# Storing the low part of the attention keys twice over, so that both products of a score contract over 128 rows

## Chip, cores, metric

One NeuronCore of a Trainium2 chip. The metric is the device time of one execution in microseconds (us), from runs of the same program; lower is better.

## What is computed

Two transformer blocks over 256 tokens of width 1024, with 256 context tokens in the first block, followed by eight routed experts. The parts that this change touches are the scores of every attention in it:

```python
# block 1, two layers: 8 query heads, 2 key heads; latents see 512 keys, context tokens 256
s = jnp.einsum('bqkgd,bskd->bkgqs', q_blk, k).astype(jnp.float32) * scale
p = jax.nn.softmax(s, axis=-1).astype(v.dtype)
# block 2, first layer (DSA): index scores choose 64 keys for each query, then attention over them
rel = jax.nn.relu(jnp.einsum('bqhd,bsd->bqhs', iqb, ik))
s = jnp.einsum('bqgrd,bqkgd->bgrqk', qg, kg).astype(F32) * scale
# block 2, second layer (NSA): compressed, selected and windowed keys, each with its own softmax
sc = jnp.einsum('bgrqd,bngd->bgrqn', qb, kc).astype(F32) * scale
ss = jnp.einsum('bgrqd,bgqnld->bgrqnl', qb, kg).astype(F32) * scale
sw = jnp.einsum('bgrqd,bkgd->bgrqk', qb, kwb).astype(F32) * scale
```

All inputs are float32 and heads are 64 wide. Everything else (projections, convolution and state scan, feed-forward layers, experts) is not changed.

## The kernel before

The program is one straight line: layer 0 and layer 1 of block 1, then the DSA layer with its feed-forward, then the NSA layer, then the experts, which run from about 1850 us to the end. Each stage streams its weights by DMA from the SP queue into `raw` tiles; ScalarE rounds a tile to float32r (L363) and VectorE subtracts to get the low part (L364), so that each float32 product is done as three float32r matmuls (L369 to L371).

Scores are done in the same spirit with two matmuls. `query_stack` puts a query's high part on rows 0 to 63 and its low part on rows 64 to 127 of one stationary tile `qS`. `put_keys` (and `keys` in `block1_mixer` for block 1) makes two tiles of key columns: `kSa`, 128 rows, the high part twice over, and `kSb`, 64 rows, the low part. For each head the first matmul (L643) contracts all 128 rows, which gives high times high plus low times high; the second (L644) takes rows 0 to 63 of the query and `kSb`, which adds high times low:

```python
nc.tensor.matmul(sb[:, j * nk:(j + 1) * nk], q, ka, start=mask is None, stop=False)
nc.tensor.matmul(sb[:, j * nk:(j + 1) * nk], q[0:64], kb, start=False,
                 stop=mask is None or j == hb - 1)
```

The same pair stands at L1302 and L1304 in `dsa` (index scores) and at L1562 and L1563 in `nsa` (scores of 16 compressed keys, with tiles `kca` and `kcb`). A pair has as many columns as the head has keys in that tile: 512, 256, 128 or 16. The heads of one bank follow each other, so the 128-row and the 64-row matmuls alternate.

After the scores of a bank VectorE takes the negated maximum of each row (L647), ScalarE the exponentials with their sums (L652), TensorE transposes the probabilities (L660), one of ScalarE and VectorE copies them out of the bank (L130, L132), and TensorE multiplies them with the values (L670). `pipeline` traces these stages some units apart, so that TensorE has other banks' work between a unit's scores and its transposes. In block 1 the units of attention are merged with those of the convolution and of the state scan; in the DSA and NSA layers they stand mostly alone.

The order of each engine's instructions is made by the tile framework's scheduler from the order of tracing; nothing around the change has a hand-made order, except that the index scores and the choice of keys (`best`, L1315 to L1321) are traced with high priority.

Of the kernel before, what the change touches and what calls it, by code (L numbers as in the profile page):

```python
# [10 lines left out]
F32 = mybir.dt.float32  # L11
# [7 lines left out]
D = 1024  # L19
# [62 lines left out]
class Split:  # L82
    """the two parts of split data, in two tiles: [:, part, ...]"""
# [8 lines left out]
class Prog:  # L92
# [41 lines left out]
    def fill(self, n=1):  # L134
        """trace the next n steps of the conditioning products; parts of a step add up"""
        self.credit += n
        while self.credit >= 1 and self.fillers:
            if next(self.fillers[0], "end") == "end":
                self.fillers.pop(0)
            self.credit -= 1  # L140
# [7 lines left out]
    def settle_fillers(self):  # L148
        """to the end of a product that has begun"""
        if self.fillers and inspect.getgeneratorstate(self.fillers[0]) == inspect.GEN_SUSPENDED:  # L150
            self.drain(self.fillers[0])

    def pipeline(self, units, lag):
        """units: lists of stages; stage j of a unit is traced some units after stage j - 1"""
# [8 lines left out]
    @staticmethod  # L163
    def along(units, step, ahead):
        """step is traced with the first stage of a unit well before the last"""
        u = units[max(0, len(units) - ahead)]
        first = u[0]

        def both():
            first()  # L170
            step()
        u[0] = both

    @staticmethod
    def merge(a, b):
        """two lists of units as one, evenly mixed"""
# [81 lines left out]
    def matvec_pe(self, w, c0, st, nd, dest, bname, boff):  # L258
        """1024 columns on the tensor engine: four column groups, two halves by the parity of k"""
# [22 lines left out]
    def matvec_dve(self, w, c0, st, nd, dest, bname, boff):  # L282
        """2048 columns for one condition or 1024 for two: products and sums over k on the vector engine,
        over partitions on the tensor engine, four column groups at once"""
# [41 lines left out]
    def in_turn(self, name, op, after=None):  # L326
        """op is issued behind the last one of the name"""
# [7 lines left out]
    def in_order(self, within=False):  # L335
        """what is traced within is issued in that order, engine by engine, behind what was traced before unless within"""
# [12 lines left out]
    def unit(self, view, a, b, raw=None, after=None):  # L349
        """a float32 weight tile [128, a * b], in DRAM or (raw) already on chip, as two float32r parts [128, a, b]"""  # L350
# [22 lines left out]
    def lin_tok(self, xT, tiles, w, n, fill=0):  # L373
        """xT(k, tile) -> (hi, lo) [128, 128]; w: [units, 128, k per unit * n] in DRAM; one bank per token tile"""
# [18 lines left out]
    def rstd(self, ss, n, inv_n):  # L393
        """[128, n] sums of squares -> (ss * inv_n + eps) ** -0.5"""
# [16 lines left out]
    def split_evac(self, hi, lo, src, scale=None, bias=None, keep=None):  # L411
        """hi, lo <- src * scale + bias, split"""
# [14 lines left out]
    def rs32(self, ss):  # L427
        """[128, 2] sums of squares of the halves of rows of D -> a 32nd of the rows' (mean square + eps) ** -0.5"""
# [14 lines left out]
    def prenorm(self, xs, dests):  # L443
        """rows of a few token tiles, with their squares in self.ssx, normalised and transposed;
        dests: (A, shift, hT, column), where the split columns times A plus shift go"""
# [25 lines left out]
    def diagonal(self, x, r=None):  # L471
        """the identity times the factors of the rows' norm"""
# [5 lines left out]
    def settle_pair(self, xs, srcs, row, post, w0):  # L478
        """settle for the two token tiles that end a stage, the diagonals for their norms and the next stage's first
        weight tile, in the order in which the engines run them"""  # L480
# [49 lines left out]
    def settle(self, x, src, row, post):  # L530
        """residual row tile x += the two halves in src, normalised when post, times the gate row; and its squares"""
# [16 lines left out]
    def slot(self):  # L548
        """16 KB per partition: half of a split input"""
        return self.hp.tile([128, 4096], F32R, name="h")  # L550

    def split_cols(self, k=8, n=512):
        """[:, part, k, column]"""
        return Split([self.slot()[:, :k * n].rearrange("p (k n) -> p k n", k=k) for _ in range(2)])

# [9 lines left out]
    def rope_tabs(self, dst, cos, sin, w=None, scale=1.0):  # L565
        """dst [128, 2, 64]: factors of x and of x with its halves swapped"""
# [10 lines left out]
    def rope(self, dst, src, H, tab, out=None):  # L577
        """src [128, H, 64] -> dst, or out, with dst as scratch"""
# [8 lines left out]
    def key_stacks(self, pool, H, n):  # L587
        return (pool.tile([128, H, n], F32R, name="kSa"), pool.tile([64, H, n], F32R, name="kSb"))

    def put_keys(self, pool, kS, d, H, t):  # L590
        """keys [128 tok, H, 64] -> columns of token tile t: high part twice over, and low part"""
        nc = self.nc
        st = pool.tile([128, H, 3, 64], F32R, name="kst")
        nc.scalar.copy(st[:, :, 0], d)
        nc.vector.tensor_sub(st[:, :, 2], d, st[:, :, 0])
        nc.vector.tensor_copy(st[:, :, 1], st[:, :, 0])
        st = st.bitcast(F32)
        pa, pb = self.bank("tr", 2), self.bank("tr", 2)
        for h in range(H):
            nc.tensor.transpose(pa[:, h * 128:h * 128 + 128], st[:, h, 0:2].rearrange("p a d -> p (a d)"), self.ident)  # L600
            nc.tensor.transpose(pb[0:64, h * 128:h * 128 + 128], st[:, h, 2], self.ident)
        sl = slice(t * 128, t * 128 + 128)
        nc.scalar.copy(kS[0][:, :, sl], pa[:, :H * 128].rearrange("p (h n) -> p h n", h=H))
        nc.vector.tensor_copy(kS[1][:, :, sl], pb[0:64, :H * 128].rearrange("p (h n) -> p h n", h=H))

    def query_stack(self, pool, d, H):
        """queries [128 tok, H, 64] -> [high; low] columns, [128, H, 128 tok]"""
# [13 lines left out]
    def attention(self, H, nk, q_of, k_of, v_of, mask, o_of, sums, finish):  # L621
        """softmax(q k) v for one tile of 128 queries and H heads: units of stages; unnormalised columns of 64 in a bank"""
# [9 lines left out]
    def attention_group(self, g, hb, nk, nkt, q_of, k_of, v_of, mask, o_of, sums):  # L632
# [3 lines left out]
        def scores():  # L636
# [4 lines left out]
            for j in range(hb):  # L641
                q, (ka, kb) = q_of(g + j), k_of(g + j)
                nc.tensor.matmul(sb[:, j * nk:(j + 1) * nk], q, ka, start=mask is None, stop=False)  # L643
                nc.tensor.matmul(sb[:, j * nk:(j + 1) * nk], q[0:64], kb, start=False,  # L644
# [29 lines left out]
    def to_mixT(self, mixT, k0, t, x, scale=None, diag=None):  # L674
        """x [128 tok, 512], times the factors of its rows in diag -> split feature columns k0..k0+3 of token tile t"""
# [18 lines left out]
    def block1_mixer(self, l, hT, mix_fill, scope):  # L694
# [16 lines left out]
        with tc.tile_pool(name=f"mix{l}", bufs=1) as big:  # L711
            xT = lambda k, t: (hT[:, 0, k, t * 128:t * 128 + 128], hT[:, 1, k, t * 128:t * 128 + 128])

            # rope tables of the two latent tiles, with the norm weights in them
# [10 lines left out]
            # q, k, v, z  # L725
# [23 lines left out]
            def keys():  # L749
# [18 lines left out]
                lo = self.wk(4, 2, 64).bitcast(F32R)  # L768
                for tp in range(2):
                    k2 = kk[:, 2 * tp:2 * tp + 2]  # L770
                    hi = self.wk(4, 2, 64).bitcast(F32R)
                    hv = hi.rearrange("p (t h) c d -> p t h c d", t=2)
                    nc.scalar.copy(hv[:, :, :, 0], k2)
                    nc.vector.tensor_sub(lo[:, 2 * tp:2 * tp + 2], k2, hv[:, :, :, 0])
                    nc.vector.tensor_copy(hi[:, :, 1], hi[:, :, 0])
                    pa, pb = self.bank("tr", 2), self.bank("tr", 2)
                    for j in range(4):
                        c = slice(128 * j, 128 * j + 128)
                        nc.tensor.transpose(pa[:, c], hi.bitcast(F32)[:, j].rearrange("p a d -> p (a d)"), self.ident)
                        nc.tensor.transpose(pb[0:64, c], lo.bitcast(F32)[:, 2 * tp + j // 2, j % 2], self.ident)  # L780
                    for copy, dst, src in ((nc.scalar.copy, kS[0], pa), (nc.vector.tensor_copy, kS[1], pb[0:64])):
# [20 lines left out]
            # x, B, C through the convolution, and dt  # L802
# [45 lines left out]
            # attention: latent queries see context and latents, context queries the context  # L848
# [51 lines left out]
    def softplus(self, d, n):  # L900
        """d [128, n] in place: max(d, 0) + log(1 + exp(-|d|)), the logarithm as 2 atanh(u / (2 + u))"""
# [14 lines left out]
    def ssd_decay(self, l, big, dv):  # L916
        """step widths, their products with A, and the exponentials of the sums of these: shared tiles, filled by steps()"""
# [28 lines left out]
    def ssd(self, l, big, xs_tok, b_tok, bT, cT, outs):  # L946
# [58 lines left out]
        def chain(i, t, first):  # L1005
            """what the incoming state adds to chunk t, and the state it leaves"""
# [67 lines left out]
    def lin_wide(self, xT, groups, w, kt, after, fill=0, between=None):  # L1074
        """groups of two token tiles of x @ w, 1024 wide, in two banks each; the last units tile by tile;
        between is traced when the first half of the first group has been"""
# [24 lines left out]
    def out_proj(self, xT, groups, w, xs, rows, post, nxt, between=None, w0=None):  # L1101
        """x @ w, normalised when post, times its gate row, added to the residual; then nxt of each group"""
# [10 lines left out]
    def gate_rows(self, pool, mod, j, w, conds):  # L1113
        """gate times w times 32, along the rows; w None: the gate alone"""
# [12 lines left out]
    def ffn(self, name, xs, hT, w_gate, w_up, w_down, row_fn, post, fills, order, nxt, need=(), w0=None):  # L1127
        """residual += gate * (norm of) swiglu; order: pairs of token tiles, as they become ready; nxt of each pair"""
# [78 lines left out]
    def positions_tables(self):  # L1207
        """cos and sin of position * frequency; the angle is brought to [-pi, pi] first"""
# [30 lines left out]
    def heads_out(self, dst, o_bank, coef, add=None):  # L1239
        """dst = o * coef per head of 64 (+ dst)"""  # L1240
# [17 lines left out]
    def dsa(self, hT):  # L1258
# [4 lines left out]
        with tc.tile_pool(name="dsa", bufs=1) as big:  # L1263
# [15 lines left out]
            with tc.tile_pool(name="dsa_i", bufs=1) as bi:  # L1279
# [12 lines left out]
                def index(t):  # L1292
                    """index scores, the 64 best keys of each query, and the mask they leave"""
# [5 lines left out]
                    for g in range(0, 8, hb):  # L1299
                        sb = self.bank()  # L1300
                        for j in range(hb):
                            nc.tensor.matmul(sb[:, j * nk:(j + 1) * nk], qS[:, g + j], ikS[0][:, 0, :nk],  # L1302
                                             start=True, stop=False)
                            nc.tensor.matmul(sb[:, j * nk:(j + 1) * nk], qS[0:64, g + j], ikS[1][:, 0, :nk],  # L1304
# [58 lines left out]
    def att_job(self, mixT, t, hf, q_of, prep, branches, first=None):  # L1363
        """eight query heads of one token tile over some branches of keys: the sum of coef * attention"""
# [30 lines left out]
    def compress(self, big, which, src):  # L1395
        """src [128, 2, 256]: tokens of four heads -> hidden units, [128, 2 (256), 4 heads, 16 blocks], in three steps"""
# [53 lines left out]
    def nsa(self, hT, ahead):  # L1450
# [5 lines left out]
        with tc.tile_pool(name="nsa", bufs=1) as big:  # L1456
            kv = [big.tile([128, 2, 512], F32, name=f"kv{i}") for i in range(3)]
            kS = [None, self.key_stacks(big, 4, 256), (big.tile([128, 4, 256], F32R, name="kSa2"),
                                                       big.tile([64, 4, 256], F32R, name="kSb2"))]
            kcS = (big.tile([128, 64], F32R, name="kca"), big.tile([64, 64], F32R, name="kcb"))  # L1460
# [24 lines left out]
            def compressed_keys():  # L1485
# [5 lines left out]
                nc.vector.tensor_sub(kcS[1], b[0:64, 0:64], kcS[0][0:64])  # L1491
# [626 lines left out]
```

## Time and profile before

| | |
|---|---|
| timed runs | 2838.80, 2838.01, 2832.42 us; median 2838.01 |
| profiled execution | span 2838.7 us, first to last instruction (the page gives no other time for it) |
| TensorE (PE) busy | 2742.1 us, 97% |
| its weight loads (PEld) | 2230.8 us, 79% |
| VectorE (DVE), ScalarE (ACT) busy | 2099.1 us (74%), 1528.1 us (54%) |
| mean granted TensorE clock | 0.959 of full speed |

PE's busy time counts a matmul from its start to the modelled end of its pipeline, and successive matmuls overlap, so 97% says that there is nearly always a matmul under way, not that the array works at its peak. The distance from one matmul's start to the next one's start tells how fast they go. The granted clock has two levels, 1.00 (2.4 GHz) and 0.50 (1.2 GHz); a stretch's number is the mean over it.

### The profile page before, as it was taken

The numbers are of one execution on the slowest core, as the hardware profiler recorded it, in microseconds if no ns is written. First come the engines' busy times: TensorE is split into PE (matmuls) and PEld (weight loads), VectorE is DVE, ScalarE is ACT, GpSimd is POOL, SyncE is SP. The second block draws the span as 40 slices with busy tenths as digits, with TensorE's granted clock in tenths as the row PEclk, the third lists the DMA queues.
The fourth block names the chain that finished last, engine by engine and source line by source line (L and its number), as shares of the span: only waits on it lengthen the run. The fifth ranks groups of instructions, "written<-read, shape, count | busy, mean of one in ns | idle before, by whom it ended". The sixth has DMA issues, their size and how long they took to land. (4 is left out here: it accounts for less than half of the span.)

```text
span 2838.7 us, 37802 instructions
## 1 busy us (share of the span) xinstructions
PE 2742.1 (97%) x13941; PEld 2230.8 (79%) x13941; DVE 2099.1 (74%) x2826; ACT 1528.1 (54%) x2255; POOL 53.0 (2%) x103
## 2 busy tenths in 40 slices
PE   7999999999999999899999999999999999999998
PEld 4767777778876898778997887788888787887876
DVE  5766677665776776656765934789999888988887
ACT  4443522323643544535444533578777777777775
POOL 0010000000001000000000000000000000000000
PEclk9999999999998999979999958899999999999999
DMA  6321567776420587422864701699899999999996
GB/s 236 112 90 31 208 219 257 268 251 206 143 89 15 177 310 235 151 68 99 301 220 151 248 12 64 209 320 355 320 349 341 334 348 341 344 344 352 347 341 243
DMA packets 180265, 641.88 MB, mean 226 GB/s; under 512 B 20621, under 2 KB 21351, under 8 KB 180071
## 3 DMA queue, kind: packets, MB, share of 16 engines
q1 hardware_dynamic: 177840, 636.05, 64.4%
q10 hardware_dynamic: 2231, 3.33, 0.4%
q8 instruction: 111, 1.82, 0.3%
q14 instruction: 83, 0.68, 0.1%
HBM read 638.25 MB, written 1.05 MB: 225 GB/s over the span
## 5 line engine op out<-in xcount | busy, mean ns | idle before, releaser
L363 ACT CAST hl<-raw 128x1024 fp32r<-128x1024 f32 (+3 forms) x1010 | 1025.5, 1033 | 656.9 <-PE mm L371 397.4
L364 DVE TENSOR_TENSOR hl<-raw,hl 128x1024 fp32r<-128x1024 f32 (+3 forms) x1010 | 1183.5, 1199 | 206.5 <-ACT hl L363 199.9
L370 PE MATMUL mm<-hl,h 128*128 128x512 f32 (+4 forms) x1616 | 630.5, 390 | 2.8 <-DVE hl L364 1.9
L371 PE MATMUL mm<-hl,h 128*128 128x512 f32 (+4 forms) x1616 | 625.2, 387 | 0.0
L369 PE MATMUL mm<-hl,h 128*128 128x512 f32 (+4 forms) x1616 | 624.1, 389 | 0.4 <-DVE wk L1160 0.3
L369 PE MATMUL mm<-h,hl 128*128 128x256 f32 (+1 forms) x1208 | 394.9, 328 | 4.8 <-DVE hl L364 4.7
L371 PE MATMUL mm<-h,hl 128*128 128x256 f32 (+1 forms) x1208 | 391.6, 324 | 0.0
L370 PE MATMUL mm<-h,hl 128*128 128x256 f32 (+1 forms) x1208 | 391.6, 324 | 0.0
L370 PEld LDWEIGHTS mm<-hl,h 128*128 128x128 f32 x1616 | 304.8, 189 | 75.5 <-DVE hl L364 10.8
L369 PEld LDWEIGHTS mm<-hl,h 128*128 128x128 f32 x1616 | 304.9, 189 | 68.9 <-ACT hl L363 2.9
L371 PEld LDWEIGHTS mm<-hl,h 128*128 128x128 f32 x1616 | 304.5, 188 | 61.8
L296 DVE SCALAR_TENSOR_TENSOR mv<-mv,st 128x1024 f32<-128x1024 f32 x154 | 196.5, 1282 | 103.1 <-DMA mv<-in_w_ada_dram 72.0
L369 PEld LDWEIGHTS mm<-h,hl 128*128 128x128 f32 x1208 | 228.4, 189 | 33.9 <-DVE hl L364 7.0
L371 PEld LDWEIGHTS mm<-h,hl 128*128 128x128 f32 x1208 | 228.7, 189 | 21.1 <-issue 1.7
L370 PEld LDWEIGHTS mm<-h,hl 128*128 128x128 f32 x1208 | 228.9, 189 | 20.3 <-issue 1.7
L370 PE MATMUL o<-hl,h 128*128 128x512 f32 x480 | 191.5, 399 | 1.3 <-DVE hl L364 0.2
L371 PE MATMUL o<-hl,h 128*128 128x512 f32 x480 | 189.1, 394 | 0.0
L369 PE MATMUL o<-hl,h 128*128 128x512 f32 x480 | 178.9, 399 | 0.0
L647 DVE TENSOR_REDUCE nmx<-mm 128x1 f32<-128x512 f32 (+2 forms) x76 | 52.4, 689 | 88.6 <-PE mm L644 86.4
L652 ACT ACTIVATE wk<-mm,nmx 128x256 f32<-128x256 f32 (+2 forms) x144 | 69.0, 488 | 81.7 <-DVE nmx L647 81.7
L370 PEld LDWEIGHTS o<-hl,h 128*128 128x128 f32 x480 | 90.3, 188 | 24.6 <-DVE hl L364 4.4
L369 PEld LDWEIGHTS o<-hl,h 128*128 128x128 f32 x480 | 90.2, 188 | 20.7 <-issue 0.8
(452 smaller groups left out, 2946.6 us busy)
## 6 DMA issues: line engine op xcount, KB each, us to landing
raw<-in_moe_w_up_dram SPq DMA_DIRECT2D x221, 512.0 KB, 5.2
raw<-in_moe_w_gate_dram SPq DMA_DIRECT2D x220, 512.0 KB, 5.5
raw<-in_moe_w_down_dram SPq DMA_DIRECT2D x219, 512.0 KB, 5.2
mv<-in_w_ada_dram SPq DMA_DIRECT2D x96, 512.0 KB, 5.0
mv<-in_w_mod_dram SPq DMA_DIRECT2D x85, 512.0 KB, 4.6
raw<-in_w_gate_dram SPq DMA_DIRECT2D x44, 512.0 KB, 4.7
raw<-in_w_up_dram SPq DMA_DIRECT2D x44, 512.0 KB, 4.5
raw<-in_w_down_dram SPq DMA_DIRECT2D x44, 512.0 KB, 3.5
```

Of the source, the lines that this page charges most:

```text
L296: nc.vector.scalar_tensor_tensor(acc, raw, st[:, k, cnd:cnd + 1], acc, op0=ALU.mult, op1=ALU.add)
L363: self.in_turn("hi", lambda: nc.scalar.copy(hl[:, 0], raw), after and after[0])
L364: self.in_turn("lo", lambda: nc.vector.tensor_sub(hl[:, 1], raw, hl[:, 0]), after and after[1])
L369: nc.tensor.matmul(out, s[1], m[0], start=start, stop=False)
L370: nc.tensor.matmul(out, s[0], m[1], start=False, stop=False)
L371: nc.tensor.matmul(out, s[0], m[0], start=False, stop=stop)
L647: nc.vector.tensor_reduce(nmx[:, :hb], sb[:, :hb * nk].rearrange("p (h k) -> p h k", h=hb), axis=AX.X, op=ALU.max, negate=True)
L652: nc.scalar.activation(pr[:, j * nk:(j + 1) * nk], sb[:, j * nk:(j + 1) * nk], AF.Exp, bias=nmx[:, j:j + 1], accum_out=sm[:, g + j:g + j + 1])
```

## The change

`kSb`, `kSb2` and `kcb` become 128 rows, with the low part of the keys on both halves, and the second matmul of each pair takes all of the query's tile. The product of the two low parts, which was left out before, is thereby in the score. To fill the tiles, ScalarE and VectorE write the duplicated halves themselves from a broadcast key, and the copy that duplicated the high part (L596, L775) is gone. The number of matmuls, their columns and the number of transposes stay as they were.

```diff
     def key_stacks(self, pool, H, n):
-        return (pool.tile([128, H, n], F32R, name="kSa"), pool.tile([64, H, n], F32R, name="kSb"))
+        return (pool.tile([128, H, n], F32R, name="kSa"), pool.tile([128, H, n], F32R, name="kSb"))
...
     def put_keys(self, pool, kS, d, H, t):
-        st = pool.tile([128, H, 3, 64], F32R, name="kst")
-        nc.scalar.copy(st[:, :, 0], d)
-        nc.vector.tensor_sub(st[:, :, 2], d, st[:, :, 0])
-        nc.vector.tensor_copy(st[:, :, 1], st[:, :, 0])
+        st = pool.tile([128, 2, H, 2, 64], F32R, name="kst")
+        d2 = d.unsqueeze(2).to_broadcast([128, H, 2, 64])
+        nc.scalar.copy(st[:, 0], d2)
+        nc.vector.tensor_sub(st[:, 1], d2, st[:, 0])
         st = st.bitcast(F32)
-        pa, pb = self.bank("tr", 2), self.bank("tr", 2)
-        for h in range(H):
-            nc.tensor.transpose(pa[:, h * 128:h * 128 + 128], st[:, h, 0:2].rearrange("p a d -> p (a d)"), self.ident)
-            nc.tensor.transpose(pb[0:64, h * 128:h * 128 + 128], st[:, h, 2], self.ident)
...
+        for i, copy in enumerate((nc.scalar.copy, nc.vector.tensor_copy)):
+            p = self.bank("tr", 2)
+            for h in range(H):
+                nc.tensor.transpose(p[:, h * 128:h * 128 + 128], st[:, i, h].rearrange("p a d -> p (a d)"), self.ident)
+            copy(kS[i][:, :, sl], p[:, :H * 128].rearrange("p (h n) -> p h n", h=H))
...
     def attention_group(...):
-                nc.tensor.matmul(sb[:, j * nk:(j + 1) * nk], q[0:64], kb, start=False,
+                nc.tensor.matmul(sb[:, j * nk:(j + 1) * nk], q, kb, start=False,
...
     block1_mixer, keys():
-                lo = self.wk(4, 2, 64).bitcast(F32R)
-                    hi = self.wk(4, 2, 64).bitcast(F32R)
-                    hv = hi.rearrange("p (t h) c d -> p t h c d", t=2)
-                    nc.scalar.copy(hv[:, :, :, 0], k2)
-                    nc.vector.tensor_sub(lo[:, 2 * tp:2 * tp + 2], k2, hv[:, :, :, 0])
-                    nc.vector.tensor_copy(hi[:, :, 1], hi[:, :, 0])
+                    hi, lo = (self.wk(4, 2, 64).bitcast(F32R) for _ in range(2))
+                    hv, lv = (x.rearrange("p (t h) c d -> p t h c d", t=2) for x in (hi, lo))
+                    for t in range(2):
+                        d2 = k2[:, t].unsqueeze(2).to_broadcast([128, 2, 2, 64])
+                        nc.scalar.copy(hv[:, t], d2)
+                        nc.vector.tensor_sub(lv[:, t], d2, hv[:, t])
...
-                        nc.tensor.transpose(pb[0:64, c], lo.bitcast(F32)[:, 2 * tp + j // 2, j % 2], self.ident)
+                        nc.tensor.transpose(pb[:, c], lo.bitcast(F32)[:, j].rearrange("p a d -> p (a d)"), self.ident)
...
     dsa, index():
-                            nc.tensor.matmul(sb[:, j * nk:(j + 1) * nk], qS[0:64, g + j], ikS[1][:, 0, :nk],
+                            nc.tensor.matmul(sb[:, j * nk:(j + 1) * nk], qS[:, g + j], ikS[1][:, 0, :nk],
...
     nsa:
-            kcS = (big.tile([128, 64], F32R, name="kca"), big.tile([64, 64], F32R, name="kcb"))
+            kcS = (big.tile([128, 64], F32R, name="kca"), big.tile([128, 64], F32R, name="kcb"))
...
-                                nc.tensor.matmul(o, qS[0:64, h], kcS[1][:, g:g + 16], start=False, stop=(h == 7))
+                                nc.tensor.matmul(o, qS[:, h], kcS[1][:, g:g + 16], start=False, stop=(h == 7))
```

The score matmuls themselves keep their places on every engine's list. What moves is the making of the key tiles. On TensorE in layer 0 of block 1, where the transposes of the keys (L779 the high part, L780 the low part) stand among the matmuls of the next projection, the list before has:

```order
L371 MATMUL mm<-hl,h 128x512
L369 MATMUL mm<-hl,h 128x512
L370 MATMUL mm<-hl,h 128x512
L371 MATMUL mm<-hl,h 128x512
L779 MATMUL tr<-cons,wk 128x128
L780 MATMUL tr<-cons,wk 64x128
L779 MATMUL tr<-cons,wk 128x128
L780 MATMUL tr<-cons,wk 64x128
```

and now:

```order
L371 MATMUL mm<-hl,h 128x512
L779 MATMUL tr<-cons,wk 128x128 x2
L369 MATMUL mm<-hl,h 128x512
L780 MATMUL tr<-cons,wk 128x128 x2
L779 MATMUL tr<-cons,wk 128x128
L780 MATMUL tr<-cons,wk 128x128
```

The first two transposes now stand three matmuls (L369 to L371) earlier, and the low part's have 128 output rows.

On VectorE in the DSA layer, the making of the key tile (`kst`, L595 and L596 before, L597 now) stands within the chain of maxima and replacements that chooses the keys of the second query tile. Before:

```order
L1315 MAX m_10108<-sc 128x8
L595 TENSOR_TENSOR kst<-h,kst 128x4x64
L1316 MATCH_REPLACE sc<-m_10108,sc 128x256
L364 TENSOR_TENSOR hl<-raw,hl 128x1024
L1315 MAX m_10108<-sc 128x8
L596 COPY kst<-kst 128x4x64
L1316 MATCH_REPLACE sc<-m_10108,sc 128x256
```

and now:

```order
L1315 MAX m_10112<-sc 128x8
L597 TENSOR_TENSOR kst<-h,kst 128x512
L1316 MATCH_REPLACE sc<-m_10112,sc 128x256
L582 TENSOR_TENSOR wk<-h,tab_122 128x4x32
L364 TENSOR_TENSOR hl<-raw,hl 128x1024
L1315 MAX m_10112<-sc 128x8
L604 CAST kSb<-tr 128x4x128
```

One subtraction of twice the width stands where a subtraction and a copy stood, and the copy into `kSb` comes earlier in the chain.

## Rows read from the trace of the kernel before

**Rows 1.** The page: busy us of each engine, share of the span, instructions.

```profile
PE 2742.1 (97%) x13941; PEld 2230.8 (79%) x13941; DVE 2099.1 (74%) x2826; ACT 1528.1 (54%) x2255; POOL 53.0 (2%) x103
```

**Rows 2.** Stretches that hold the scores: span, busy per engine, clock, DMA share.

```profile
850.00:925.00 75.00, 68.42 (x333) 49.75 (x332) 46.38 (x81) 26.88 (x56) 9.40 (x12) 0.82 0.05 15
...
1657.00:1700.00 43.00, 43.00 (x170) 36.47 (x169) 12.46 (x35) 12.05 (x52) 0.00 (x0) 0.56 0.00 1
1700.00:1730.00 30.00, 29.99 (x186) 23.58 (x185) 15.00 (x30) 14.09 (x46) 0.00 (x0) 1.00 0.00 1
...
sum 503.00, PE 482.87 PEld 366.93 DVE 285.14 ACT 207.38 POOL 28.94; mean PE 40.24 PEld 30.58 DVE 23.76 ACT 17.28 POOL 2.41
```

**Rows 3.** Instructions on kSb and kcb: count, ns min/median/max, forms.

```profile
L644 PE MATMUL mm<-kSb,qS x144: 322/472/792, 112.2 to 1760.5; 64*128 64x256 f32 x64, 64*128 64x128 f32 x48, 64*128 64x512 f32 x32
L1304 PE MATMUL mm<-kSb,qS x16: 323/382/579, 1205.1 to 1225.0; 64*128 64x128 f32 x8, 64*128 64x256 f32 x8
...
L1563 PE MATMUL mm<-kcb,qS x32: 273/273/379, 1635.8 to 1729.2; 64*128 64x16 f32 x32
```

**Rows 4.** Timeline, 512 columns, layer 0: start us, us, engine, line.

```profile
111.62 0.39 PE L371 MATMUL mm<-h,hl 128*128 128x512 f32 x1
111.62 0.19 PEld L643 LDWEIGHTS mm<-kSa,qS 128*128 128x128 f32 x1
111.85 0.40 PE L643 MATMUL mm<-kSa,qS 128*128 128x512 f32 x1
...
112.17 0.18 PEld L644 LDWEIGHTS mm<-kSb,qS 64*128 64x128 f32 x1 [0.36 <-issue]
...
112.60 0.50 PE L369 MATMUL mm<-h,hl 128*128 128x512 f32 x1
```

**Rows 5.** Timeline of PE, 256 columns at full clock, NSA layer.

```profile
1710.68 0.38 PE L643 MATMUL mm<-kSa,qS 128*128 128x256 f32 x1
...
1711.31 0.38 PE L1664 MATMUL tr<-cons,affine 128*128 128x128 f32 x1
```

**Rows 6.** Timeline of PE, 256 columns, 128 rows throughout (a projection).

```profile
1350.08 0.28 PE L370 MATMUL mm<-h,hl 128*128 128x256 f32 x1
1350.19 0.28 PE L371 MATMUL mm<-h,hl 128*128 128x256 f32 x1
```

**Rows 7.** Timeline of PE, 128 columns at half clock, NSA layer.

```profile
1668.36 0.47 PE L644 MATMUL mm<-kSb,qS 64*128 64x128 f32 x1
...
1669.17 0.47 PE L644 MATMUL mm<-kSb,qS 64*128 64x128 f32 x1
...
1670.38 1.97 PE L670 MATMUL o<-kv,wk 128*128 128x64 f32 x8
1672.10 0.77 PE L639 MATMUL mm<-causr,identr 128*128 128x512 f32 x1
```

**Rows 8.** Timeline of PE, 16 columns at full clock, NSA layer.

```profile
1657.86 0.28 PE L1562 MATMUL mm<-kca,qS 128*128 128x16 f32 x1
...
1658.27 0.28 PE L1562 MATMUL mm<-kca,qS 128*128 128x16 f32 x1
```

**Rows 9.** L644 by stretch of one clock: span, PE and PEld busy (count), clock, DMA.

```profile
1259.30:1276.40 17.10, 3.78 (x8) 2.28 (x8) 0.50 0.03 12
...
1638.20:1655.30 17.10, 7.07 (x15) 4.32 (x15) 0.50 0.00 1
...
1662.10:1699.60 37.50, 7.54 (x16) 4.54 (x16) 0.50 0.00 1
...
1730.30:1750.80 20.50, 4.63 (x8) 2.28 (x8) 0.50 0.00 0
```

**Rows 10.** Instructions on kst: the making of the key tiles.

```profile
L596 DVE CAST kst<-kst x8: 185/279/289, 1187.6 to 1630.9; 128x256 fp32r<-128x256 f32 x6, 128x64 fp32r<-128x64 f32 x2
L594 ACT CAST kst<-kv x4: 402/406/410, 1574.9 to 1630.1; 128x256 fp32r<-128x256 f32 x4
L595 DVE TENSOR_TENSOR kst<-kv,kst x4: 406/416/425, 1575.9 to 1630.5; 128x256 fp32r<-128x256 f32 x4
```

More of the change, by code (lines that the diff above doesn't have):

```diff
@@ L587, in key_stacks @@
     def key_stacks(self, pool, H, n):
-        return (pool.tile([128, H, n], F32R, name="kSa"), pool.tile([64, H, n], F32R, name="kSb"))
+        return (pool.tile([128, H, n], F32R, name="kSa"), pool.tile([128, H, n], F32R, name="kSb"))
     def put_keys(self, pool, kS, d, H, t):
         nc = self.nc
-        st = pool.tile([128, H, 3, 64], F32R, name="kst")
-        nc.scalar.copy(st[:, :, 0], d)
-        nc.vector.tensor_sub(st[:, :, 2], d, st[:, :, 0])
-        nc.vector.tensor_copy(st[:, :, 1], st[:, :, 0])
+        st = pool.tile([128, 2, H, 2, 64], F32R, name="kst")
+        d2 = d.unsqueeze(2).to_broadcast([128, H, 2, 64])
+        nc.scalar.copy(st[:, 0], d2)
+        nc.vector.tensor_sub(st[:, 1], d2, st[:, 0])
         st = st.bitcast(F32)
-        pa, pb = self.bank("tr", 2), self.bank("tr", 2)
-        for h in range(H):
-            nc.tensor.transpose(pa[:, h * 128:h * 128 + 128], st[:, h, 0:2].rearrange("p a d -> p (a d)"), self.ident)
-            nc.tensor.transpose(pb[0:64, h * 128:h * 128 + 128], st[:, h, 2], self.ident)
         sl = slice(t * 128, t * 128 + 128)
-        nc.scalar.copy(kS[0][:, :, sl], pa[:, :H * 128].rearrange("p (h n) -> p h n", h=H))
-        nc.vector.tensor_copy(kS[1][:, :, sl], pb[0:64, :H * 128].rearrange("p (h n) -> p h n", h=H))
+        for i, copy in enumerate((nc.scalar.copy, nc.vector.tensor_copy)):
[3 more added lines that the diff above has]
+            copy(kS[i][:, :, sl], p[:, :H * 128].rearrange("p (h n) -> p h n", h=H))
     def query_stack(self, pool, d, H):
@@ L779, in keys @@
                         nc.tensor.transpose(pa[:, c], hi.bitcast(F32)[:, j].rearrange("p a d -> p (a d)"), self.ident)
-                        nc.tensor.transpose(pb[0:64, c], lo.bitcast(F32)[:, 2 * tp + j // 2, j % 2], self.ident)
-                    for copy, dst, src in ((nc.scalar.copy, kS[0], pa), (nc.vector.tensor_copy, kS[1], pb[0:64])):
+                        nc.tensor.transpose(pb[:, c], lo.bitcast(F32)[:, j].rearrange("p a d -> p (a d)"), self.ident)
+                    for copy, dst, src in ((nc.scalar.copy, kS[0], pa), (nc.vector.tensor_copy, kS[1], pb)):
                         copy(dst[:, :, 256 * tp:256 * tp + 256].rearrange("p h (t n) -> p t h n", t=2),
@@ L1458, in nsa @@
             kS = [None, self.key_stacks(big, 4, 256), (big.tile([128, 4, 256], F32R, name="kSa2"),
-                                                       big.tile([64, 4, 256], F32R, name="kSb2"))]
-            kcS = (big.tile([128, 64], F32R, name="kca"), big.tile([64, 64], F32R, name="kcb"))
+                                                       big.tile([128, 4, 256], F32R, name="kSb2"))]
+            kcS = (big.tile([128, 64], F32R, name="kca"), big.tile([128, 64], F32R, name="kcb"))
             mixT = self.slot().rearrange("p (a k n) -> p a k n", a=2, k=8)
@@ L1490, in compressed_keys @@
                 nc.scalar.copy(kcS[0], b[:, 0:64])
-                nc.vector.tensor_sub(kcS[1], b[0:64, 0:64], kcS[0][0:64])
+                nc.vector.tensor_sub(kcS[1], b[:, 0:64], kcS[0])
             def compressed_values():
```

## The prediction

> **What bounds the kernel now.** I read the page first, then the stretches that hold the scores, then single matmuls there, start by start. [rows 1] say that TensorE is busy for 2742 of 2838.7 us and the next engine, VectorE, for 2099: the kernel is bound by TensorE wherever no wait says otherwise. [rows 2] ask that of the attention itself: over twelve stretches of 503 us TensorE is busy for 482.87 (96%), VectorE for 285, ScalarE for 207. In the NSA layer, 1657 to 1730 us, it is busy without a gap while VectorE has 29 to 50% of the time and ScalarE 28 to 47%. Those two wait for TensorE there, not it for them. DMA's share in that layer is 0.00, so the experts' weights can't run ahead while it lasts, and whatever the layer loses, all that comes behind it loses too.
>
> So the question is how TensorE spends its time there. In [rows 4] each matmul starts 0.23 us behind the one before it (111.62, 111.85) as long as all have 128 rows, and the weight load of the next starts together with the matmul that runs. The 64-row matmul breaks this: its load starts only at 112.17, after 0.36 us in which the loader stood idle, and the 128-row one behind it starts at 112.60. From 111.85 to 112.60 the pair took 0.75 us where two steps of 0.23 make 0.46. The number of rows changes twice in a pair, and each time TensorE empties before it goes on. [rows 3] count the pairs: 144 in the attentions (32 of 512 columns, 64 of 256, 48 of 128), 16 of the index scores (8 of 256, 8 of 128) and 32 of 16 columns, 192 in all.
>
> **The change, part by part.** Its main part makes every matmul of the scores a 128-row one. I take from each pair what it has over two 128-row steps of the same columns.
>
> - 512 columns: 0.75 - 0.46 = 0.29 us [rows 4]; 32 pairs make 9.3 us. A few of them run at half clock, which I leave aside.
> - 256 columns at full clock: from 1710.68 to 1711.31 a pair is 0.63 us [rows 5], two 128-row steps are 0.24 (0.12 each, between 1350.08 and 1350.19) [rows 6]; 0.39 us. Of 64 pairs 8 lie in a half-clock stretch [rows 9], so 56 x 0.39 = 21.8 us.
> - The 8 at half clock have no row here. The ends are 0.39, were emptying independent of the clock, and 0.78, were all of it twice as long; I take 0.5, nearer to the first: 4.0 us.
> - 128 columns at half clock: from 1668.36 to 1669.17 a pair is 0.81 us [rows 7]. What two 128-row steps of 128 columns would take, the trace shows for eight matmuls on 128 rows that change weights every time: 1670.38 to 1672.10, 0.215 each. So 0.81 - 0.43 = 0.38 us. [rows 9] have 8 + 15 + 16 = 39 such pairs: 14.8 us. For the 9 at full clock I take the middle between the gains of 16 and 256 columns (0.19 and 0.39), 0.29: 2.6 us.
> - 16 columns: 0.41 us a pair [rows 8]. The step can't be less than the weights take to change; half of the 0.215 at half clock is 0.11, as an estimate. 0.41 - 0.22 = 0.19, times 32 is 6.1 us.
> - Index scores: 8 x 0.39 + 8 x 0.29 = 5.4 us.
>
> The sum is 64.0 us of TensorE's own time. Since it is busy for 96% of these stretches [rows 2], I count 96% of it on the path: **61 us**. The emptiest is layer 1 of block 1, 68.42 of 75 us, with few pairs; the fullest, NSA, has the most.
>
> The second part is the clock. Four stretches in the DSA and NSA layers run at 0.50, 17.1 + 17.1 + 37.5 + 20.5 = 92.2 us [rows 9], and the stretch between the last two, which has the same kind of work on 256 keys, at 1.00 [rows 2]. The longest begins at 1662.10, right behind the 16-column pairs of [rows 8], when TensorE had had mostly short streams and emptyings. Taking the emptyings out (14.8 + 4.0 of the 92.2) leaves 73 us at half clock. Were all that at full clock, half of it would go, 37 us. The same streams will stand closer together, and the 16-column stretches, ahead of one of the falls, are halved; against that, a faster TensorE may come to wait for the exponentials. The ends are thus a gain of 37 and a loss: were the full-clock stretch of 1700 to 1730 us to fall too, its 30 us less 6 of emptying would take some 24 us more. I take a gain of **15 us**, two fifths of the upper end, since TensorE is the engine without gaps there.
>
> The third part is the key tiles. ScalarE's rounding and VectorE's subtraction go from 256 to 512 elements a row, at most twice 0.41 and 0.42 us, and the copy of 0.28 goes [rows 10]: per tile up to 0.41 more on ScalarE and 0.14 on VectorE, ten tiles in all (six here, four pieces in block 1) and two small ones. That is 4 us of ScalarE and 1.4 of VectorE spread over five places, beside projections that keep TensorE busy; bounds on the path are a gain (the transposes of the high part no longer wait for subtraction and copy, 0.7 us a tile) and 5 us lost if TensorE waits for each. The transposes that stand three matmuls earlier (0.7 us) may wait that long twice. In the DSA layer the wider subtraction stands in the chain that chooses the keys of the second query tile, whose mask is wanted only behind the first tile's attention: 0.14 us, hidden. The transposes' steps are set by 128 columns as before. On SP a few loads of the NSA projections change places, same tiles and bytes: nothing. I take **1 us** lost.
>
> Together 61 + 15 - 1 = 75: from the profiled span of 2838.7 that gives 2763.7, and against the median of 2838.0, 0.7 lower, **2763 us**.
>
> **The rivals.**
> - *The clock comes back wholly* in the four stretches: 61 + 37 - 1 = 97, so 2741 us, and less if part of layer 1 (0.82 in [rows 2]) joins in. For it: the neighbouring stretch at 1.00. Against: the 128-key units have the least streaming for each wait. The Trainium skill, "TensorE: Matmul & The Clock Gate", section "What's actually happening", says that throttled is the default and that activity releases it; the trace agrees as far as dense projections stand at 1.00, and by that rule this rival is the right end. 0.17.
> - *The softmax chain takes over.* With the emptyings gone, scores, maximum, exponentials, transposes follow each other faster than ScalarE and VectorE answer, and TensorE waits. The chain can matter only in DSA and NSA, where units stand alone, some 43 of the 64 us (all but 512 columns, the 16 pairs of 256 in layer 0 and the index scores). If half of those are lost and the clock gives nothing: 61 - 21 - 1 = 39, so 2799 us. Against: ScalarE has 14.09 of 30 us in the full-clock stretch [rows 2], and taking out 6.2 us leaves it 59% busy. 0.10.
> - *Slower: the clock falls in layers 0 and 1 of block 1*, where it stands near full now. It would take TensorE waiting there for VectorE, busy 46.38 of 75 us. Layer 1's 75 us at 0.82 are 27 us at half and 48 at full clock, so falling wholly would cost it up to 48 us, and a stretch of like length in layer 0 up to 75; it decides from the point where more than 60 us of full clock are lost. If both fall, the time is 2838 - 60 + 48 + 75 = 2901 us. Nothing in the profile speaks for it but the gaps of layer 1. 0.03.
> - *The step isn't the rows' doing*: the exposed load comes from something that stays, such as two products in one group on the same query. Then nothing is gained and the key tiles cost 1 to 3: about 2840 us. Against: L369 to L371 also add products into one bank and step at 0.23 [rows 4]. The Trainium skill, "TensorE: Matmul & The Clock Gate", section "What overlaps and what doesn't", says that a weight load overlaps a running matmul only when their row groups differ; by that rule 128-row pairs could not overlap either and the gain would be nil. The trace shows the contrary, a 128-row load and a 128-row matmul both starting at 111.62. 0.03.
>
> **How the numbers follow.** The forecast, 2748 to 2785, has the remaining 0.67. The range that should hold 8 in 10 runs from 2733, below the full return of the clock with some of layer 1, to 2799, the softmax chain's end. A measurement of this kernel can tell about 0.3%, 8.5 us, from no change. The first two rivals are faster too: 0.67 + 0.17 + 0.10 = 0.94, and 0.01 of the third. The rest is 0.03 for no change (most of the fourth) and 0.02 for slower.
>
> **What would show it.** In the changed profile a 128-row L644 should start 0.12 us behind L643 at 256 columns and 0.23 at 512, the 16-column pair should take about 0.22, and the loads of L644 should start with the matmul before. The NSA layer's work between 1638.20 and 1750.80 [rows 9], 112.6 us, should take 70 to 85. Clock rows at 1.00 throughout it would show the first rival; idle TensorE ahead of L660, with waits for L652, the second; a clock of 0.50 in the attention of layer 0 the third; an unchanged step of 0.31 at 256 columns the fourth, and with it the prediction would be wrong from its first term.

## The result, and the profile after

The changed kernel takes 2752.8 us (median; 2747.6 to 2753.7) against 2838.4 for the one before beside it: a ratio of 0.9694, 95% interval 0.9677 to 0.9710, so 86 us less. The forecast was 2763 us, within 2733 to 2799.

On the page of the changed kernel the busy times answer to [rows 1]:

```profile
PE 2644.2 (96%) x13941; PEld 2178.2 (79%) x13941; DVE 2100.7 (76%) x2818; ACT 1529.1 (56%) x2259; POOL 52.7 (2%) x103
```

TensorE has lost 98 us of busy time with the same 13941 matmuls; VectorE and ScalarE have kept theirs. The instructions on `kSb`, as in [rows 3], have the same counts with 128 rows:

```profile
L644 PE MATMUL mm<-kSb,qS x144: 272/282/628, 113.0 to 1672.5; 128*128 128x256 f32 x64, 128*128 128x128 f32 x48, 128*128 128x512 f32 x32
```

Single pairs in its timeline (start us, us, engine, line). First 512 columns in layer 0, against [rows 4]:

```profile
112.55 0.39 PE L371 MATMUL mm<-h,hl 128*128 128x512 f32 x1
112.55 0.19 PEld L643 LDWEIGHTS mm<-kSa,qS 128*128 128x128 f32 x1
112.78 0.39 PE L643 MATMUL mm<-kSa,qS 128*128 128x512 f32 x1
112.78 0.19 PEld L644 LDWEIGHTS mm<-kSb,qS 128*128 128x128 f32 x1
...
113.01 0.40 PE L644 MATMUL mm<-kSb,qS 128*128 128x512 f32 x1
...
113.24 0.39 PE L369 MATMUL mm<-h,hl 128*128 128x512 f32 x1
```

The load of L644 now starts together with the matmul ahead of it (both at 112.78), and the pair takes 0.46 us (112.78 to 113.24) where it took 0.75. Then 256 columns in the NSA layer, against [rows 5]:

```profile
1640.55 0.28 PE L643 MATMUL mm<-kSa,qS 128*128 128x256 f32 x1
1640.67 0.28 PE L644 MATMUL mm<-kSb,qS 128*128 128x256 f32 x1
1640.79 0.28 PE L643 MATMUL mm<-kSa,qS 128*128 128x256 f32 x1
...
1641.03 0.33 PE L670 MATMUL o<-kv,wk 128*128 128x64 f32 x2
```

That is 0.24 us a pair, 0.63 before. The first pair of a bank, which [rows 5] leave out, was cheaper before, 0.52 us (1710.16 to 1710.68), and takes 0.24 now as well:

```profile
1710.16 0.28 PE L643 MATMUL mm<-kSa,qS 128*128 128x256 f32 x1
```

Sixteen columns at full clock, against [rows 8]:

```profile
1613.24 0.26 PE L1562 MATMUL mm<-kca,qS 128*128 128x16 f32 x1
1613.35 0.26 PE L1563 MATMUL mm<-kcb,qS 128*128 128x16 f32 x1
1613.46 0.26 PE L1562 MATMUL mm<-kca,qS 128*128 128x16 f32 x1
```

0.22 a pair, 0.41 before. At 128 columns and half clock, against [rows 7], from one L644 to the next it is 0.43 (0.81 before):

```profile
1605.11 0.41 PE L644 MATMUL mm<-kSb,qS 128*128 128x128 f32 x1
1605.32 0.41 PE L643 MATMUL mm<-kSa,qS 128*128 128x128 f32 x1
1605.54 0.41 PE L644 MATMUL mm<-kSb,qS 128*128 128x128 f32 x1
```

Where the time went by layer is read from stretches between the first and the last score (span, busy times of PE, PEld, DVE, ACT and POOL, clock, DMA). Before: layer 0, layer 1, DSA with its index scores, NSA:

```profile
111.00:269.00 158.00, 154.15 (x852) 111.33 (x850) 108.84 (x174) 67.84 (x143) 18.73 (x28) 1.00 0.24 81
805.00:922.00 117.00, 110.42 (x542) 83.67 (x541) 75.88 (x119) 46.54 (x90) 9.93 (x20) 0.87 0.10 32
1204.00:1298.00 94.00, 91.16 (x404) 70.52 (x402) 52.73 (x130) 41.27 (x109) 0.66 (x1) 0.82 0.18 56
1635.60:1760.50 124.90, 124.87 (x552) 99.07 (x552) 45.88 (x108) 45.08 (x164) 0.00 (x0) 0.70 0.05 18
```

After:

```profile
112.00:263.00 151.00, 145.83 (x854) 111.80 (x853) 109.21 (x174) 67.90 (x143) 19.03 (x28) 0.99 0.25 84
805.00:911.00 106.00, 98.54 (x542) 80.08 (x543) 76.51 (x119) 46.46 (x91) 9.62 (x20) 0.92 0.12 35
1192.00:1263.00 71.00, 64.87 (x401) 54.97 (x400) 52.60 (x128) 40.61 (x105) 0.34 (x1) 0.95 0.23 74
1600.40:1672.60 72.20, 71.82 (x552) 67.24 (x553) 45.25 (x108) 44.85 (x164) 0.00 (x0) 0.93 0.08 31
```

NSA went from 124.9 to 72.2 us, DSA from 94 to 71, layer 1 from 117 to 106, layer 0 from 158 to 151. The clock rose from 0.70 to 0.93 in NSA and from 0.82 to 0.95 in DSA. These four gains add up to 94 us, and the profiled span fell by 87: in this one profile layer 1 starts at 805 us both times, so that layer 0's 7 us had been lost on the way. The last experiments are about that.

### The profile page after: what moved, and what is told of

Same layout as the page of the kernel before. It is cut to its first block, busy times and chain, and to the rows that moved or that the text cites. A ratio compares the mean times of both kernels' runs of the same rounds, so it can differ in the third digit from the quotient of the medians.

```text
span 2751.8 us, 37805 instructions
## 1 busy us (share of the span) xinstructions
PE 2644.2 (96%) x13941; PEld 2178.2 (79%) x13941; DVE 2100.7 (76%) x2818; ACT 1529.1 (56%) x2259; POOL 52.7 (2%) x103
## 3 DMA queue, kind: packets, MB, share of 16 engines
HBM read 638.25 MB, written 1.05 MB: 232 GB/s over the span
## 5 line engine op out<-in xcount | busy, mean ns | idle before, releaser
L371 PE MATMUL mm<-hl,h 128*128 128x512 f32 (+4 forms) x1616 | 626.3, 388 | 0.0
L369 PE MATMUL mm<-hl,h 128*128 128x512 f32 (+4 forms) x1616 | 623.8, 389 | 1.1 <-DVE wk L1160 0.8
L369 PE MATMUL mm<-h,hl 128*128 128x256 f32 (+1 forms) x1208 | 394.5, 327 | 6.0 <-DVE hl L364 5.9
L371 PE MATMUL mm<-h,hl 128*128 128x256 f32 (+1 forms) x1208 | 390.9, 324 | 0.0
L369 PEld LDWEIGHTS mm<-hl,h 128*128 128x128 f32 x1616 | 304.9, 189 | 69.8 <-ACT hl L363 3.0
L371 PEld LDWEIGHTS mm<-hl,h 128*128 128x128 f32 x1616 | 304.8, 189 | 61.4
L369 PEld LDWEIGHTS mm<-h,hl 128*128 128x128 f32 x1208 | 228.2, 189 | 35.1 <-DVE hl L364 10.8
L371 PEld LDWEIGHTS mm<-h,hl 128*128 128x128 f32 x1208 | 228.0, 189 | 21.1 <-issue 1.7
L371 PE MATMUL o<-hl,h 128*128 128x512 f32 x480 | 189.1, 394 | 0.0
L369 PE MATMUL o<-hl,h 128*128 128x512 f32 x480 | 178.9, 399 | 0.0
L370 PEld LDWEIGHTS o<-hl,h 128*128 128x128 f32 x480 | 90.3, 188 | 24.7 <-DVE hl L364 4.4
L369 PEld LDWEIGHTS o<-hl,h 128*128 128x128 f32 x480 | 90.2, 188 | 20.7 <-issue 0.8
L371 PEld LDWEIGHTS o<-hl,h 128*128 128x128 f32 x480 | 90.3, 188 | 19.6
L652 ACT ACTIVATE wk<-mm,nmx 128x256 f32<-128x256 f32 (+2 forms) x144 | 69.1, 491 | 55.6 <-DVE nmx L647 55.4
```

The lines of the kernel that those rows point to most:

```text
L369: nc.tensor.matmul(out, s[1], m[0], start=start, stop=False)
L370: nc.tensor.matmul(out, s[0], m[1], start=False, stop=False)
L371: nc.tensor.matmul(out, s[0], m[0], start=False, stop=stop)
L652: nc.scalar.activation(pr[:, j * nk:(j + 1) * nk], sb[:, j * nk:(j + 1) * nk], AF.Exp, bias=nmx[:, j:j + 1], accum_out=sm[:, g + j:g + j + 1])
```

## The experiments

**1. The making of the key tiles alone.** The second product is put back on 64 rows; the tiles are made as in the change.

```diff
-nc.tensor.matmul(sb[:, j * nk:(j + 1) * nk], q, kb, start=False,
+nc.tensor.matmul(sb[:, j * nk:(j + 1) * nk], q[0:64], kb[0:64], start=False,
```

(and the same for the index scores and the 16-column scores). The product of the two low parts drops out of the scores with it.

> The changed kernel with its key tiles made as changed, but the second product of every score on rows 0 to 63 again. Theory (all of the gain is the matmuls' rows, the making of the key tiles costs nothing that shows): back to 2838 us, within 4; L644 at 256 columns again 0.31 us behind L643. Rival (part of the gain comes from the other order and the copies that went): it stays below 2830.

Measured: 2839.7 us against 2840.0, ratio 1.0010 (0.9994 to 1.0026). The gain is the matmuls' rows; the tiles' making and its other order are worth nothing that shows (the interval is 2 us faster to 7 us slower).

**2. Fewer changes of rows, with all 64-row products kept.** In the kernel before, in banks with a mask and in the 16-column scores (the edit is shortened here):

```diff
 for j in range(hb):
     nc.tensor.matmul(sb[:, j * nk:(j + 1) * nk], q, ka, start=False, stop=False)
-    nc.tensor.matmul(sb[:, j * nk:(j + 1) * nk], q[0:64], kb, ...)
+for j in range(hb):
+    nc.tensor.matmul(sb[:, j * nk:(j + 1) * nk], q[0:64], kb, ...)
```

> The kernel before, 64-row products kept, but in each bank of masked scores (DSA and NSA) and of the 16-column scores all 128-row products first, then all 64-row ones. Theory (the price is paid at each change of the number of rows): the changes fall from 96 to 48 for 256 columns, 96 to 24 for 128, 64 to 8 for 16; with 0.19, 0.18 and 0.095 us each that is 9 + 13 + 5 = 27 us, and up to 15 more from the clock: 2796 to 2811 us. Rival (the price belongs to each 64-row product): no change, 2838.

Measured: 2800.9 us, ratio 0.9864 (0.9834 to 0.9895), 39 us less. In its timeline of TensorE a bank of two heads is:

```profile
1681.04 0.40 PE L643 MATMUL mm<-kSa,qS 128*128 128x256 f32 x2
1681.37 0.50 PE L648 MATMUL mm<-kSb,qS 64*128 64x256 f32 x2
1681.80 1.10 PE L673 MATMUL o<-kv,wk 128*128 128x64 f32 x8
```

0.76 us for the four products, which took 1.15 before (1710.16 to 1711.31). Eight 64-row products of 16 columns in a row take 1.05 us from the first start to the last end, so they follow each other at about 0.11 us, as those of 128 rows do in the changed kernel:

```profile
1624.40 1.05 PE L1569 MATMUL mm<-kcb,qS 64*128 64x16 f32 x8
```

The price is at the change, not in the 64-row product itself. 27 us were counted for the changes. The other 12 are put down to the clock, by difference; in the NSA stretch of this run it stood at 0.79 (0.70 before):

```profile
1623.20:1718.70 95.50, 95.49 (x550) 82.30 (x550) 45.65 (x108) 45.12 (x164) 0.00 (x0) 0.79 0.07 23
```

**3. The 16-column scores alone put back to 64 rows** in the changed kernel:

```diff
-nc.tensor.matmul(o, qS[:, h], kcS[1][:, g:g + 16], start=False, stop=(h == 7))
+nc.tensor.matmul(o, qS[0:64, h], kcS[1][0:64, g:g + 16], start=False, stop=(h == 7))
```

> The changed kernel with the 64-row product in the 16-column scores of the compressed keys alone. Changes of rows: 64 x 0.095 = 6 us, so 2759 us if nothing else follows. Theory (these stretches are where the clock falls, and shortening them kept it up): the clock falls behind them more often again, up to 15 us more, 2759 to 2774, with more of the NSA layer at 0.50 than in the changed kernel. Rival (the clock rose because the 128- and 256-key products stand closer): 2759 and no more time at 0.50.

Measured: 2767.6 us, ratio 0.9744 (0.9704 to 0.9783): 15 us more than the changed kernel, where 6 were counted for the changes of rows; its four runs spread from 2756 to 2773 us. The NSA layer has four stretches of such scores, each ahead of other products. The last 16-column products of the second, third and fourth stretch, and the stretches at half clock that follow:

```profile
1615.82 0.27 PE L1563 MATMUL mm<-kcb,qS 64*128 64x16 f32 x1
...
1640.56 0.32 PE L1563 MATMUL mm<-kcb,qS 64*128 64x16 f32 x1
...
1667.97 0.38 PE L1563 MATMUL mm<-kcb,qS 64*128 64x16 f32 x1
```

```profile
1616.80:1633.80 17.00, 17.00 (x80) 16.61 (x79) 6.26 (x17) 5.62 (x23) 0.00 (x0) 0.50 0.00 1
1640.70:1644.10 3.40, 3.40 (x16) 3.38 (x17) 0.86 (x5) 0.59 (x1) 0.00 (x0) 0.50 0.00 0
1668.00:1674.80 6.80, 6.80 (x33) 6.68 (x33) 3.17 (x7) 1.57 (x5) 0.00 (x0) 0.50 0.00 0
```

All three are followed by a fall within 1 us. In the changed kernel the work behind the same three runs at full clock:

```profile
1614.90:1627.00 12.10, 11.92 (x103) 11.51 (x103) 6.86 (x22) 7.05 (x31) 0.00 (x0) 1.00 0.01 1
1632.30:1654.00 21.70, 21.69 (x180) 20.50 (x180) 15.16 (x34) 12.48 (x38) 0.00 (x0) 1.00 0.00 1
1656.50:1672.60 16.10, 16.10 (x135) 15.27 (x135) 12.37 (x29) 10.88 (x39) 0.00 (x0) 1.00 0.35 132
```

Within or just behind the first stretch it falls in both kernels. In this profile the changed kernel has one more fall in NSA, 12 us behind the second stretch and soon after sixteen transposes of 8 columns:

```profile
1624.92 1.92 PE L1652 MATMUL tr<-wr,moda 128*128 128x8 f32 x16
```

```profile
1627.10:1630.50 3.40, 3.40 (x14) 2.26 (x11) 2.26 (x5) 2.09 (x9) 0.00 (x0) 0.50 0.00 0
```

**4. The same part alone**: everything on 64 rows as in the first experiment, only the 16-column scores on 128.

> The run with all second products on 64 rows, but the 16-column scores of the compressed keys on 128 rows: this part of the change alone. Changes of rows taken out: 6 us. Theory (these stretches make the clock fall): 6 us and 6 to 20 more, 2814 to 2828 us, with fewer falls right behind them. Rival (with the 64-row products of the selected and windowed keys around them the clock falls anyhow): 2834.

Measured: 2821.0 us, ratio 0.9942 (0.9921 to 0.9963), 11 to 22 us for 6 us of changes. The NSA stretch shrinks to 101.9 us at a clock of 0.83, from 127.1 at 0.68 in the first experiment (the profiled run, 2809.3 us, is the fastest of its seven). The first experiment, then this one:

```profile
1632.20:1759.30 127.10, 127.10 (x551) 101.12 (x551) 45.93 (x108) 45.32 (x164) 0.00 (x0) 0.68 0.05 18
```

```profile
1627.50:1729.40 101.90, 101.89 (x553) 80.97 (x552) 45.82 (x108) 45.33 (x164) 0.00 (x0) 0.83 0.06 22
```

So these scores on 64 rows bring the clock down even with the other products as they were. They are not the only thing that does: in this run it still falls at 1654.5 us, 6 us behind the last 16-column product, amid selected scores on 128 and 64 rows in turn:

```profile
1654.50:1674.90 20.40, 20.40 (x73) 16.51 (x74) 6.36 (x15) 6.69 (x29) 0.00 (x0) 0.50 0.00 1
```

**5. DSA alone put back**, attention and index scores.

> The changed kernel with the 64-row product in the DSA layer, index scores and attention. Theory: the changes of rows there (11 us in the attention, 6 in the index scores) and the clock, whose half-speed time there was 34 us before and 7 after: 17 us and 4 to 10 more, 2774 to 2780 us. Rival (the choice of keys on VectorE bounds the index part, so that its share is hidden): 2764 to 2770.

Measured: 2771.0 us, ratio 0.9772 (0.9746 to 0.9798): 18 us behind the changed kernel's median, 22 by the two ratios, and its stretch is 94.3 us at 0.80. The median lies 3 us below the theory's range and 1 us above the rival's, so it decides nothing; the profile's stretch fits the theory. That the choice of keys hides part of the loss is not shown.

**6. Layers 0 and 1.** Three edits put back, or leave, one layer by a flag that `block1` sets:

```diff
+                if self.narrow:
+                    q, kb = q[0:64], kb[0:64]
                 nc.tensor.matmul(sb[:, j * nk:(j + 1) * nk], q, kb, start=False,
```

Layer 0 alone back to 64 rows:

> The changed kernel with the 64-row product in layer 0 of block 1 alone. Theory (what layer 0 gained is lost again behind it, where the conditioning weights' transfers bound the program): within 1 us of 2753, with the lead of 6 us at 500 us gone by 610 us in both. Rival (layer 0 counts on the path by its 11 us): 2759 to 2764.

Measured: 2755.1 us, ratio 0.9698 (0.9667 to 0.9729), 2 us from the changed kernel, between what the theory and the rival had expected. It seemed that layer 0 is worth next to nothing. Both layers back:

> The changed kernel with the 64-row product in both layers of block 1. Theory: layer 0 is worth nothing, layer 1 its 16 pairs of 0.29, 5 us: 2758 us. Rival (the 11 us by which layer 1 drew ahead in the profiles are the change's): 2764 or more.

Measured: 2762.6 us, ratio 0.9738 (0.9712 to 0.9764): 10 us for both, again between the two. Five were expected of layer 1, so the rest spoke for layer 0. Three more runs, taken side by side ("the third experiment" in the next text is the first run of this experiment, layer 0 alone back):

> All second products on 64 rows except those of layer 0 of block 1: this layer's part alone. By its terms it is worth 0.29 x 16 + 0.39 x 16 = 11 us. Theory (two later profiles with 128 rows in layer 0 keep a lead of 7 to 10 us up to layer 1, against the one of the changed kernel that lost it near 600 us): 5 to 10 us faster than before, 2828 to 2833. Rival (the conditioning weights' transfers behind it bound the program, as the third experiment seemed to say): within 2 us of before.

> The changed kernel with the 64-row product in layer 0 alone, again, beside the changed kernel itself in the same call. Theory: slower than it by 5 to 10 us. Rival: by less than 3.

> The changed kernel itself, for comparison with the other two in the same call: 2753 us, within 5.

Measured: layer 0's part alone 2831.1 us, ratio 0.9967 (0.9950 to 0.9983), 11 us less than before (5 to 14); in the changed kernel, put back, 2761.7 (0.9719, 0.9699 to 0.9739) against 2747.3 (0.9672, 0.9651 to 0.9692) for the changed kernel beside it, 14 us. So the first reading was wrong: layer 0 does count. That reading rested on the changed kernel's first runs, which are 5 us slower in the median than these, and on their one profile, in which the clock fell once within layer 0's attention (0.99 above). In the second profile it did not, and between the same two matmuls the kernel before took 157.3 us:

```profile
111.50:259.30 147.80, 143.12 (x850) 110.02 (x849) 108.96 (x173) 67.57 (x143) 19.00 (x28) 1.00 0.26 86
```

```profile
111.80:269.10 157.30, 153.45 (x848) 110.67 (x847) 108.94 (x174) 67.94 (x143) 18.73 (x28) 1.00 0.25 81
```

That is 9.5 of the 11 us counted. The 14 us are more; one reason may be that in the profile of layer 0 put back the clock fell there, too:

```profile
113.60:277.20 163.60, 159.74 (x848) 114.96 (x846) 109.08 (x174) 68.05 (x143) 18.73 (x28) 0.96 0.23 78
```

Layer 1's own worth no pair of runs settles; it varies between profiles of like products. From its first score to its last the six profiles with 128 rows there have 106 to 112 us, 109 in the mean, and the six with 64 rows 111 to 118, 113 in the mean: some 4 us, where 5 were counted.

## Why the prediction was right

- **What bounds the kernel.** TensorE, as read from [rows 1, 2]. It still does: in NSA it is busy for 71.82 of 72.2 us.
- **The price of a change of rows.** The steps behind [rows 4, 5, 7, 8] came out as forecast: 0.46, 0.24, 0.43 and 0.22 us for pairs of 512, 256, 128 (half clock) and 16 columns, where the same four were put in. Experiment 2 shows that it is paid at the change. The 61 us counted are some 3 too many: half of the 56 pairs of 256 columns at full clock are the first of their bank and gain 0.28 us (0.52 less 0.24), not 0.39.
- **The clock.** This is the term that was mis-sized, 15 us, taken as two fifths of an upper end of 37. In NSA the terms for the changes make 12 + 13 + 6 = 31 us (31 half-clock and one full-clock pair of 128 columns; 24 at full clock and 8 at half of 256; all of 16), and the layer lost 52.7: about 21 are left for the clock. In DSA with its index scores, 16 of 23 us are changes, some 7 the clock's. That makes about 28, by difference. The sign set for the NSA layer shows the same: its work of 1638.20 to 1750.80 was to take 70 to 85 us and takes 64:

```profile
1601.70:1665.70 64.00, 63.62 (x483) 59.22 (x484) 39.40 (x97) 38.18 (x145) 0.00 (x0) 0.92 0.01 1
```

The measured 86 lie half-way between the forecast's 75 and the 97 of the clock's whole return. Two things were missing. The upper end left out the index scores, which ran at 0.66 before and at 1.00 now:

```profile
1204.80:1225.40 20.60, 19.88 (x66) 14.71 (x66) 4.78 (x21) 4.76 (x9) 0.00 (x0) 0.66 0.09 33
```

```profile
1192.60:1203.00 10.40, 9.43 (x66) 8.33 (x66) 3.42 (x14) 4.39 (x9) 0.00 (x0) 1.00 0.19 65
```

And it was not known which work made the clock fall: the 16-column stretches, named in the prediction for one of the falls only. Experiments 3 and 4 show that they are one such work, in NSA. DSA has none of them, and with its own products back on 64 rows its clock is at 0.80 again (experiment 5; 0.82 before, 0.95 in the changed kernel).
- **The key tiles.** The forecast was 1 us lost; none shows, though experiment 1 can't tell 1 us from none. On ScalarE the rounding takes 0.62 us where 0.82 was the bound, on VectorE the subtraction 0.68 where it was 0.83, against [rows 10]:

```profile
L596 ACT CAST kst<-kv x4: 615/620/623, 1539.8 to 1595.7; 128x512 fp32r<-128x512 f32 x4
L597 DVE TENSOR_TENSOR kst<-kv,kst x4: 683/684/693, 1540.8 to 1596.3; 128x512 fp32r<-128x512 f32 x4
```

- **The rivals.** The softmax chain did not take over: in NSA TensorE has no gaps to speak of. In DSA it is now busy for 64.87 of 71 us (91.16 of 94 before), so some 3 us are lost there, and that is this chain: TensorE waits for the exponentials (L652) for 4.1 us, where it was 1.5 before (us, times, longest; before, then after):

```profile
PE mm L639 <- ACT wk L652: 1.5, 1, 1.5
```

```profile
PE mm L639 <- ACT wk L652: 4.1, 2, 3.8
```

3.8 of them are one wait, up to 1237.02, and within it the clock fell to half for 6.8 us:

```profile
1237.02 0.80 PE L639 MATMUL mm<-mask,identr 128*128 128x512 f32 x1 [3.82 <-ACT wk L652]
```

```profile
1234.60:1241.40 6.80, 4.38 (x18) 3.70 (x19) 3.58 (x8) 4.70 (x20) 0.00 (x0) 0.50 0.15 57
```

The clock did not fall in layers 0 and 1 at large. That the step is not the rows' doing fell with experiment 1: the same tiles and order, with the rows put back, give the time of before.

That the tile making alone costs nothing that shows, that the changes carry the price and that the 16-column stretches bring the clock down is shown by runs. How the 86 us divide into changes and clock is counted, not shown. The selected and windowed products of NSA were not run alone; by difference (86 less about 11 for layer 0, 15 for the 16-column scores, 18 for DSA and up to 5 for layer 1) they hold the largest share, some 40 us. So the forecast was 11 us short: the clock gave about 13 us more than it said, the changes some 3 less, and these two errors partly offset each other.

## What to carry to other kernels

Where TensorE is the bound, compare the distance of successive matmul starts with that of a like pair elsewhere in the same trace; here a weight load that no longer started together with the matmul ahead (112.17 in [rows 4]) marked the place. Filling unused rows with something harmless or useful, so that all matmuls in a row use the same number, cost these matmuls nothing (0.24 us a pair of 256 columns, as in a projection), and where that can't be done, grouping those of one size gets part of it (39 of 86 us). And look at what stands just ahead of each fall of the clock: the 16-column scores on 64 rows cost 15 us here, where their own changes of rows were counted at 6.

## What the runs showed that was not expected

In experiment 3 each of the four stretches of sixteen 16-column matmuls, half of them on 64 rows, takes 3.3 to 4.0 us, and the clock fell within it or less than 1 us behind it. In the changed kernel they take 1.9 to 2.3 us, and it fell so behind the first alone. And one profile misled: in it layer 0 kept 2 to 3 us less of its gain, with a single fall of the clock, and that the rest was gone by layer 1 looked like a bound by transfers. Starts of layer 1 in later profiles of kernels with 128 rows in layer 0 lay at 795.8 to 801.8 us, of those with 64 rows at 803.7 to 816.4.
